# Hybrid decoder step: memory attention of the sampled sequences, eight sequences of a head in one step instead of four

## The chip, the cores and the metric

The kernel runs on one core of a Trainium2 chip. A time is the device time of one execution in microseconds; the comparison is of medians over several executions. The profile is of one execution of its own. Engines are called PE (matrix products), DVE (vector), ACT (scalar, activations), POOL and SP (here only an issuer of DMAs).

## What is computed

One decoding step of a two-layer decoder for two request groups with the same weights: one prompt of 512 tokens and eight sampled sequences of 8 tokens. Each layer has a mixer, a cross-attention into 256 memory tokens, and a feed-forward part. The change touches the cross-attention of the sampled group (`q` is 8 x 8 x 4 heads x 256, `k` and `v` are caches of 8 x 256 x 4 x 256, one for each sequence):

```python
def mem_attend(h, k, v, w_q, w_o):
    B, T, _ = h.shape
    q = (h @ w_q).reshape(B, T, MEM_HEADS, MEM_HEAD_DIM)
    s = jnp.einsum('bthe,bnhe->bhtn', q, k, preferred_element_type=F32) * MEM_HEAD_DIM ** -0.5
    p = jax.nn.softmax(s, axis=-1)
    o = jnp.einsum('bhtn,bnhe->bthe', p, v.astype(F32)).reshape(B, T, D_MODEL).astype(h.dtype)
    return o @ w_o
# in every layer
xp = xp + mem_attend(rmsnorm(xp, g_mem_q[layer]), mk, mv, w_mem_q[layer], w_mem_o[layer])
xs = xs + mem_attend(rmsnorm(xs, g_mem_q[layer]), cache_mem_k[layer], cache_mem_v[layer],
                     w_mem_q[layer], w_mem_o[layer])
```

## The kernel before, in words

The whole step is one program. The prompt's 512 columns and the samples' 64 stand side by side, so that the dense products (`dense`, line 922) run over 256 and 320 columns (`HALF`, line 32). A dense weight comes as a raw 128x1024 tile `wr`; ACT casts its high part `wh`, DVE subtracts the low part `wl` (`low_now`, line 891), and each product is made of three matmuls (`wh` twice, `wl` once). There are two raw buffers (`NR`, line 709): the load of the weight after next (`load_to`, line 857) is issued on SP's queue and waits there until DVE has made the `wl` of two weights earlier, which reads the same buffer.

The memory stage `mem_stage` (line 1891) runs once in each layer. The planner `sched` (line 802) writes its instructions in one order for all engines. Into the dense product of Q (the filler) and then the dense product of the output (`o`, which waits in the planner until all parts of its head are in `fin`), it lays three lanes, piece by piece: the prompt's attention in two halves (`mem_prompt`, line 1927, four heads each), and the samples' attention (`mem_sample`, line 1974), a chain of eight steps: four heads, two blocks of four sequences each. PE takes its instructions in exactly the written order, and so does each other engine. The numbers that a piece yields are its estimated time on PE and until its next piece may follow.

One step of `mem_sample` takes four K tiles; makes S in one PSUM bank, with four sequences side by side in groups of 32 rows (8 matmuls of 256 columns); takes the row maximum on DVE; the exponential on ACT; turns P on PE and copies it out; takes four V tiles; makes P V (8 matmuls); scales on ACT; turns the result back; and splits it for the output product.

K and V come through a `_Stream` (line 440): a list of sources (`mem_src`, line 1923, K of a block then V of it) from which tiles of 128x512 (256 KB) are loaded on SP's queue, up to eight ahead (`get`, `fill`), but a further one only where the arena has more than `MROOM` = 4500 columns of room left (line 308). Tiles lie in regions of large pages, which get new owners when the old tile is deleted: a load waits on SP until the last reader of its region is done. All DMAs of the stage go through SP's queue in the written order.

Of the kernel before, what the change touches and what calls it, by code (L numbers as in the profile page):

```python
# [11 lines left out]
AF = mybir.ActivationFunctionType  # L12
OP = mybir.AluOpType
AX = mybir.AxisListType
# [293 lines left out]
MROOM = 4500  # L308
# [393 lines left out]
class _Prog:  # L702
# [1188 lines left out]
    def mem_stage(self, l, nx):  # L1891
        nc = self.nc
        Q = self.wide("mq", dt=F32)
        oh, ol = self.wide("xh"), self.wide("xl")
        done = set()

        def ev(i, hf, ps):
            t0, N = HALF[hf]
            nx.upto(hf)
            nc.vector.tensor_tensor(Q[i][:, t0:t0 + N], ps[:, :N], nx.R[:, t0:t0 + N], op=OP.mult)  # L1900
            done.add((i, hf))
            if len(done) == 2 * KT:
                nx.clear()

        q = lambda: self.dense(self.pos[f"mq{l}"], 8, KT, nx.h, nx.l, ev, first=6)

        fin = set()
        st = _Stream(self, [s for h in range(4) for k in range(2) for s in self.mem_src(l, h, k)], "Kb", 8, MROOM)
        lanes = [self.chain(*[self.mem_prompt(l, h, hf, Q, done, oh, ol, fin) for h in range(4)]) for hf in range(2)]
        lanes.append(self.chain(*[self.mem_sample(l, h, b, Q, done, st, oh, ol, fin) for h in range(4) for b in range(2)]))  # L1910
        nn = _Next(self, "g_ffn", l * 8)
        ready = lambda k: lambda: sum((k // 2, j) in fin for j in ("a0", "a1", "s0", "s1")) == 4

        def o():
            yield 0, 0, lambda: len(done) == 2 * KT
            yield from self.dense(self.pos[f"mo{l}"], 8, KT, oh, ol, self.res_evac(nn), first=6, ready=ready)

        f = self.sched(lanes + [o()], q(), METM)
        assert f is None or next(f, None) is None
        self.Kc[l], self.Vc[l] = None, None  # L1920
        return nn

    def mem_src(self, l, h, blk):
        b = range(blk * 4, blk * 4 + 4)
        return [self.aps["cmk"][l, i, h] for i in b] + [self.aps["cmv"][l, i, h] for i in b]

    def mem_prompt(self, l, h, hf, Q, done, oh, ol, fin):
        nc = self.nc
# [42 lines left out]
        fin.add((h, f"a{hf}"))  # L1971
        yield 1.7, 0

    def mem_sample(self, l, h, blk, Q, done, st, oh, ol, fin):

        nc = self.nc
        yield 0, 0, lambda: (2 * h, 1) in done and (2 * h + 1, 1) in done
        q0 = 512 + 32 * blk
        mx, den = self.T([128, 1], "mx"), self.T([128, 1], "den")
        Kb = [st.get() for _ in range(4)]  # L1980
        ps = self.PS()
        for eh in range(2):
            for j in range(4):
                c = q0 + 8 * j - 24
                nc.tensor.matmul(ps[32 * j:32 * j + 32, :256], Q[2 * h + eh][:, c:c + 32],
                                 Kb[j][:, eh * 256:eh * 256 + 256], start=eh == 0, stop=eh == 1)
        del Kb
        nc.vector.tensor_reduce(mx[:], ps[:, :256], axis=AX.X, op=OP.max)
        nc.vector.tensor_scalar(mx[:], mx[:], -1.0 / 16, None, op0=OP.mult)
        yield 1.0, 1.0  # L1990
        p_ = self.S([128, 256], s="P")
        nc.scalar.activation(p_[:], ps[:, :256], AF.Exp, bias=mx[:], scale=1.0 / 16, accum_out=den[:])
        del ps
        yield 0, 0.9
        ps = self.PS()
        for kt in range(2):
            nc.tensor.transpose(ps[:, kt * 128:kt * 128 + 128], p_[:, kt * 128:kt * 128 + 128], self.ident)
        pt = self.S([128, 256], s="PT")
        nc.vector.reciprocal(den[:], den[:])
        nc.vector.tensor_copy(pt[:], ps[:, :256])  # L2000
        yield 0.22, 1.2
        Vb = [st.get() for _ in range(4)]
        O = self.PS()
        for kt in range(2):
            for j in range(4):
                nc.tensor.matmul(O[32 * j:32 * j + 32, :256], pt[:, kt * 128 + 32 * j:kt * 128 + 32 * j + 32],
                                 Vb[j][:, kt * 256:kt * 256 + 256], start=kt == 0, stop=kt == 1)
        del Vb
        o = self.S([128, 256], s="O")
        nc.scalar.activation(o[:], O[:, :256], AF.Copy, scale=den[:])  # L2010
        yield 1.0, 1.2
        ps = self.PS()
        for vh in range(2):
            nc.tensor.transpose(ps[:, vh * 128:vh * 128 + 128], o[:, vh * 128:vh * 128 + 128], self.ident)
        for vh in range(2):
            i = 2 * h + vh
            v = lambda a: a.rearrange("p (j c) -> p j c", j=4)
            src = v(ps[:, vh * 128:vh * 128 + 128])[:, :, 24:32]
            self.split(src, v(oh[i][:, q0:q0 + 32]), v(ol[i][:, q0:q0 + 32]))
        fin.add((h, f"s{blk}"))  # L2020
        yield 0.22, 0


    def ffn(self, l, nx, nn):
# [476 lines left out]
```

## Time and profile before

| what | value |
|---|---|
| three runs | 2065.84, 2068.98, 2069.39 us; median 2068.98 us |
| the profiled execution | 2069.16 us, of which the span of its instructions is 2067.4 us |
| PE, DVE, ACT busy | 97%, 61%, 39% of the span |
| the chain that ended last | PE 87%, DVE 6%, DMA 3%, ACT 3% |
| mean granted TensorE clock | 0.989 of full speed |
| K and V tiles of the memory stages | 128 loads of 256 KB, 5.2 us (K) and 4.9 us (V) from issue to landing |

All instructions are recorded in one helper line, L630, so rows are told apart by tiles: `page,wh` and `page,wl` are dense products, `page,page 128*32` are the samples' S or P V (a row of 16 records is the eight matmuls of a group), `page,page 128*128` the prompt's, and `cid,page` the turnings. A timeline row gives its start, its length and in brackets the idle time before it. Rows overlap a little at their ends, so that the time of a group is better read from its start to the next row's start. SPq is SP's queue of DMA issues.

### The profile page before, as it was taken

The page shows a single profiled execution, that of the slowest core. Times are in us where ns is not written, and L with a number is a line of the kernel's source. Part 1 is how long each engine was busy: PE and PEld are TensorE (multiplying, and loading weights), DVE is VectorE, ACT ScalarE, POOL GpSimd, SP SyncE. Part 2 cuts the span into 40 slices and gives each one's busy share as a digit, 9 for nine tenths or more (in the row PEclk, how much of TensorE's full clock was granted, in tenths as well). Part 3 has the DMA queues.
Part 4 walks back from the last instruction along what each step waited for, and adds up shares of the span by engine and source line. Part 5 has one row for each costly group of instructions (what it writes and reads, how often), then busy time and mean ns, then how long its engine had stood idle before and what let it go on. Part 6 is the DMA issues. An engine that isn't in the chain of part 4 may idle for free.

```text
span 2067.4 us, 40636 instructions
## 1 busy us (share of the span) xinstructions
PE 2010.5 (97%) x16443; PEld 1860.1 (90%) x16443; DVE 1259.5 (61%) x3020; ACT 801.3 (39%) x1674; POOL 264.6 (13%) x570
## 2 busy tenths in 40 slices
PE   7999999999999999999999999999999999999997
PEld 6999867978999999999898878878879999999996
DVE  7785676643677377377426666655645675575575
ACT  5554434333444244144322342344434443343342
POOL 1142120000012012020003212200000021121111
PEclk9999999999999999999999999999999999999998
DMA  4222145555222222222555555566453222222222
GB/s 150 69 65 73 54 123 190 189 184 186 79 83 82 82 82 82 83 83 88 156 185 169 181 178 194 182 205 199 168 190 113 79 82 86 85 86 83 82 70 77
DMA packets 104092, 252.30 MB, mean 122 GB/s; under 512 B 11169, under 2 KB 22049, under 8 KB 103905
## 3 DMA queue, kind: packets, MB, share of 16 engines
q1 hardware_dynamic: 103760, 249.49, 37.1%
q8 instruction: 129, 2.11, 0.4%
q14 instruction: 59, 0.48, 0.1%
q10 hardware_dynamic: 144, 0.22, 0.0%
HBM read 227.70 MB, written 21.96 MB: 121 GB/s over the span
## 4 chain that ended last, share of the span: by engine, by line
PE 87%; DVE 6%; DMA 3%; ACT 3%; issue 1%; POOL 0%; SPq 0%; DVEq 0%; ACTq 0%; POOLq 0%
PE p L630 87%; DVE page L630 4%; ACT page L630 2%; DMA wr<-in_w 1%; DVE wl L630 1%; ACT wh L630 1%; DMA page<-in_cmk 1%; DVE rn L630 1%; DMA out_o_ss<-page 0%; DMA page<-xd 0%; DMA page<-in_x 0%; POOL page L630 0%; SPq L630 0%; DMA xd<-page 0%; DVE ot L630 0%
## 5 line engine op out<-in xcount | busy, mean ns | idle before, releaser
L630 PE MATMUL p<-page,wh 128*128 128x256 f32 (+1 forms) x7296 | 1103.1, 299 | 17.6 <-ACT wh L630 12.8
L630 PEld LDWEIGHTS p<-page,wh 128*128 128x128 f32 x7296 | 1012.9, 191 | 45.9 <-issue 20.6
L630 PE MATMUL p<-page,wl 128*128 128x256 f32 (+1 forms) x3648 | 589.7, 298 | 0.0
L630 PEld LDWEIGHTS p<-page,wl 128*128 128x128 f32 x3648 | 519.7, 191 | 14.0 <-issue 13.1
L630 DVE TENSOR_TENSOR page<-p,page 128x256 f32<-128x256 f32 (+5 forms) x647 | 242.1, 392 | 320.0 <-PE p L630 233.2
L630 ACT CAST wh<-wr 128x1024 fp32r<-128x1024 f32 (+1 forms) x268 | 275.6, 1031 | 391.9 <-PE p L630 313.6
L630 DVE TENSOR_TENSOR wl<-wr,wh 128x1024 fp32r<-128x1024 f32 (+1 forms) x268 | 332.9, 1245 | 83.5 <-ACT wh L630 76.7
L630 DVE SCALAR_TENSOR_TENSOR page<-page,vecs,page 128x256 f32<-128x256 f32 (+4 forms) x545 | 283.9, 526 | 97.7 <-ACT page L630 86.8
L630 PE MATMUL p<-page,page 64*64 64x64 f32 (+12 forms) x3778 | 296.7, 298 | 11.5 <-DVE page L630 4.0
L630 PEld LDWEIGHTS p<-page,page 128*32 128x32 f32 (+6 forms) x3778 | 191.1, 130 | 80.1 <-issue 30.4
L630 ACT ACTIVATE page<-page,vecs 128x256 f32<-128x256 f32 (+5 forms) x319 | 169.1, 539 | 229.7 <-DVE page L630 223.7
L630 POOL COPY page<-page 128x16 f32<-128x16 f32 (+5 forms) x312 | 128.6, 438 | 731.2 <-DVE page L630 731.2
L630 ACT ACTIVATE page<-page 128x256 f32<-128x256 f32 (+6 forms) x293 | 116.2, 412 | 139.0 <-DVE page L630 132.7
L630 POOL TENSOR_TENSOR page<-page,page 128x256 f32<-128x256 f32 (+6 forms) x93 | 90.1, 976 | 463.1 <-DVE page L630 325.9
L630 ACT COPY page<-p 128x256 f32<-128x256 f32 (+8 forms) x161 | 63.9, 413 | 186.2 <-PE p L630 185.3
L630 PE MATMUL p<-wh,page 128*128 128x512 f32 (+1 forms) x368 | 119.1, 397 | 0.0
L630 DVE TENSOR_TENSOR page<-page,page 128x256 fp32r<-128x256 f32 (+8 forms) x178 | 80.1, 462 | 57.8 <-ACT page L630 56.8
L630 DVE TENSOR_TENSOR page<-page 128x256 f32<-128x256 f32 (+5 forms) x225 | 99.4, 454 | 16.3 <-POOL page L630 11.1
L630 ACT CAST page<-page 128x256 fp32r<-128x256 f32 (+2 forms) x118 | 50.4, 442 | 125.7 <-DVE page L630 125.7
L630 PEld LDWEIGHTS p<-wh,page 128*128 128x128 f32 (+1 forms) x368 | 77.3, 223 | 14.4 <-issue 2.5
L630 PE MATMUL p<-cid,page 128*128 128x128 f32 (+3 forms) x669 | 79.4, 258 | 5.7 <-ACT page L630 4.0
L630 POOL MEMSET page<- 128x2 f32 (+4 forms) x110 | 12.2, 112 | 539.2 <-PE p L630 290.1
(84 smaller groups left out, 827.5 us busy)
## 6 DMA issues: line engine op xcount, KB each, us to landing
wr<-in_w SPq DMA_DIRECT2D x252, 512.0 KB, 3.6
page<-in_ck SPq DMA_DIRECT2D x72, 256.0 KB, 4.6
page<-in_cv SPq DMA_DIRECT2D x72, 256.0 KB, 4.2
page<-in_cmk SPq DMA_DIRECT2D x64, 256.0 KB, 5.2
page<-in_cmv SPq DMA_DIRECT2D x64, 256.0 KB, 4.9
wr<-in_w SPq DMA_DIRECT2D x16, 384.0 KB, 3.1
xd<-page SPq DMA_DIRECT2D x16, 288.0 KB, 4.3
out_o_v<-page SPq DMA_DIRECT2D x12, 256.0 KB, 4.3
```

Of the source, the lines that this page charges most:

```text
L630: return f(*args, **kw)
```

## The change

The two blocks of a head become one step. `mem_sample` takes eight K tiles, then makes both blocks' S in the two halves of one PSUM bank (16 matmuls), with one maximum of 128x2 over 512 columns, two exponentials, four turnings in place of two and a copy of 512 columns; then it takes eight V tiles and makes both blocks' P V (16 matmuls), two scaled copies, four turnings and a split of 64 columns. The stream's order becomes eight K then eight V for each head, in place of four and four; `ahead` and `MROOM` stay. The output product waits in the planner for one part `s` instead of `s0` and `s1`. PE has as many instructions as before; DVE has 48 fewer and ACT 16 fewer; SP has as many DMAs.

```diff
--- before.py
+++ after.py
@@ -1905,11 +1905,11 @@
         q = lambda: self.dense(self.pos[f"mq{l}"], 8, KT, nx.h, nx.l, ev, first=6)
 
         fin = set()
-        st = _Stream(self, [s for h in range(4) for k in range(2) for s in self.mem_src(l, h, k)], "Kb", 8, MROOM)
+        st = _Stream(self, [s for h in range(4) for s in self.mem_src(l, h)], "Kb", 8, MROOM)
         lanes = [self.chain(*[self.mem_prompt(l, h, hf, Q, done, oh, ol, fin) for h in range(4)]) for hf in range(2)]
-        lanes.append(self.chain(*[self.mem_sample(l, h, b, Q, done, st, oh, ol, fin) for h in range(4) for b in range(2)]))
+        lanes.append(self.chain(*[self.mem_sample(l, h, Q, done, st, oh, ol, fin) for h in range(4)]))
         nn = _Next(self, "g_ffn", l * 8)
-        ready = lambda k: lambda: sum((k // 2, j) in fin for j in ("a0", "a1", "s0", "s1")) == 4
+        ready = lambda k: lambda: sum((k // 2, j) in fin for j in ("a0", "a1", "s")) == 3
 
         def o():
             yield 0, 0, lambda: len(done) == 2 * KT
@@ -1920,9 +1920,8 @@
         self.Kc[l], self.Vc[l] = None, None
         return nn
 
-    def mem_src(self, l, h, blk):
-        b = range(blk * 4, blk * 4 + 4)
-        return [self.aps["cmk"][l, i, h] for i in b] + [self.aps["cmv"][l, i, h] for i in b]
+    def mem_src(self, l, h):
+        return [self.aps["cmk"][l, i, h] for i in range(8)] + [self.aps["cmv"][l, i, h] for i in range(8)]
 
     def mem_prompt(self, l, h, hf, Q, done, oh, ol, fin):
         nc = self.nc
@@ -1971,54 +1970,64 @@
         fin.add((h, f"a{hf}"))
         yield 1.7, 0
 
-    def mem_sample(self, l, h, blk, Q, done, st, oh, ol, fin):
+    def mem_sample(self, l, h, Q, done, st, oh, ol, fin):
+
 
         nc = self.nc
         yield 0, 0, lambda: (2 * h, 1) in done and (2 * h + 1, 1) in done
-        q0 = 512 + 32 * blk
-        mx, den = self.T([128, 1], "mx"), self.T([128, 1], "den")
-        Kb = [st.get() for _ in range(4)]
+        mx, den = self.T([128, 2], "mx"), self.T([128, 2], "den")
+        Kb = [st.get() for _ in range(8)]
         ps = self.PS()
-        for eh in range(2):
-            for j in range(4):
-                c = q0 + 8 * j - 24
-                nc.tensor.matmul(ps[32 * j:32 * j + 32, :256], Q[2 * h + eh][:, c:c + 32],
-                                 Kb[j][:, eh * 256:eh * 256 + 256], start=eh == 0, stop=eh == 1)
+        for b in range(2):
+            for eh in range(2):
+                for j in range(4):
+                    c = 512 + 32 * b + 8 * j - 24
+                    nc.tensor.matmul(ps[32 * j:32 * j + 32, b * 256:b * 256 + 256], Q[2 * h + eh][:, c:c + 32],
+                                     Kb[4 * b + j][:, eh * 256:eh * 256 + 256], start=eh == 0, stop=eh == 1)
         del Kb
-        nc.vector.tensor_reduce(mx[:], ps[:, :256], axis=AX.X, op=OP.max)
+        nc.vector.tensor_reduce(mx[:], ps[:].rearrange("p (b n) -> p b n", b=2), axis=AX.X, op=OP.max)
         nc.vector.tensor_scalar(mx[:], mx[:], -1.0 / 16, None, op0=OP.mult)
-        yield 1.0, 1.0
-        p_ = self.S([128, 256], s="P")
-        nc.scalar.activation(p_[:], ps[:, :256], AF.Exp, bias=mx[:], scale=1.0 / 16, accum_out=den[:])
+        yield 2.0, 1.2
+        p_ = self.S([128, 512], s="P")
+        for b in range(2):
+            c = slice(b * 256, b * 256 + 256)
+            nc.scalar.activation(p_[:, c], ps[:, c], AF.Exp, bias=mx[:, b:b + 1], scale=1.0 / 16, accum_out=den[:, b:b + 1])
         del ps
-        yield 0, 0.9
+        yield 0, 1.2
         ps = self.PS()
-        for kt in range(2):
-            nc.tensor.transpose(ps[:, kt * 128:kt * 128 + 128], p_[:, kt * 128:kt * 128 + 128], self.ident)
-        pt = self.S([128, 256], s="PT")
+        for n in range(4):
+            nc.tensor.transpose(ps[:, n * 128:n * 128 + 128], p_[:, n * 128:n * 128 + 128], self.ident)
+        pt = self.S([128, 512], s="PT")
         nc.vector.reciprocal(den[:], den[:])
-        nc.vector.tensor_copy(pt[:], ps[:, :256])
-        yield 0.22, 1.2
-        Vb = [st.get() for _ in range(4)]
+        nc.vector.tensor_copy(pt[:], ps[:])
+        del p_
+        yield 0.44, 1.2
+        Vb = [st.get() for _ in range(8)]
         O = self.PS()
-        for kt in range(2):
-            for j in range(4):
-                nc.tensor.matmul(O[32 * j:32 * j + 32, :256], pt[:, kt * 128 + 32 * j:kt * 128 + 32 * j + 32],
-                                 Vb[j][:, kt * 256:kt * 256 + 256], start=kt == 0, stop=kt == 1)
+        for b in range(2):
+            for kt in range(2):
+                for j in range(4):
+                    c = b * 256 + kt * 128 + 32 * j
+                    nc.tensor.matmul(O[32 * j:32 * j + 32, b * 256:b * 256 + 256], pt[:, c:c + 32],
+                                     Vb[4 * b + j][:, kt * 256:kt * 256 + 256], start=kt == 0, stop=kt == 1)
         del Vb
-        o = self.S([128, 256], s="O")
-        nc.scalar.activation(o[:], O[:, :256], AF.Copy, scale=den[:])
-        yield 1.0, 1.2
+        o = self.S([128, 512], s="O")
+        for b in range(2):
+            c = slice(b * 256, b * 256 + 256)
+            nc.scalar.activation(o[:, c], O[:, c], AF.Copy, scale=den[:, b:b + 1])
+        yield 2.0, 1.2
         ps = self.PS()
         for vh in range(2):
-            nc.tensor.transpose(ps[:, vh * 128:vh * 128 + 128], o[:, vh * 128:vh * 128 + 128], self.ident)
+            for b in range(2):
+                nc.tensor.transpose(ps[:, vh * 256 + b * 128:vh * 256 + b * 128 + 128],
+                                    o[:, b * 256 + vh * 128:b * 256 + vh * 128 + 128], self.ident)
         for vh in range(2):
             i = 2 * h + vh
-            v = lambda a: a.rearrange("p (j c) -> p j c", j=4)
-            src = v(ps[:, vh * 128:vh * 128 + 128])[:, :, 24:32]
-            self.split(src, v(oh[i][:, q0:q0 + 32]), v(ol[i][:, q0:q0 + 32]))
-        fin.add((h, f"s{blk}"))
-        yield 0.22, 0
+            v = lambda a: a.rearrange("p (j c) -> p j c", j=8)
+            src = v(ps[:, vh * 256:vh * 256 + 256])[:, :, 24:32]
+            self.split(src, v(oh[i][:, 512:576]), v(ol[i][:, 512:576]))
+        fin.add((h, "s"))
+        yield 0.44, 0
 
 
     def ffn(self, l, nx, nn):
```

What it moves, first on SP in head 1 of layer 0. `page_3939` and `page_4197` are the pages with the stream's regions, `wr_…` the raw weights. Before:

```order
L630 DMA wr_4793<-in_w 128x1024
L630 DMA wr_4806<-in_w 128x1024
L630 DMA page_3939<-in_cmk 128x512 x3
L630 DMA page_3939<-in_cmv 128x512 x4
L630 DMA page_4197<-in_cmk 128x512
L630 DMA wr_4975<-in_w 128x1024
L630 DMA page_3939<-in_cmk 128x512 x3
L630 DMA page_3939<-in_cmv 128x512 x4
L630 DMA page_4197<-in_cmk 128x512
```

After:

```order
L630 DMA wr_4808<-in_w 128x1024
L630 DMA page_3939<-in_cmk 128x512 x7
L630 DMA page_4197<-in_cmk 128x512
L630 DMA page_4197<-in_cmv 128x512
L630 DMA wr_4970<-in_w 128x1024
L630 DMA page_3939<-in_cmv 128x512 x7
L630 DMA wr_5047<-in_w 128x1024
```

Before, three K and four V tiles stand between two weight loads, for blocks that come later. Now eight K tiles of head 1 stand ahead of the first V tile of that head, the load of `wr_4970` comes next, and the head's other seven V tiles behind it.

DVE at the same place: `mx` is the row maximum (`mx_4910` and `mx_4928` that of the samples), `wl_4858` and `wl_4882` the low part whose raw buffer `wr_4970` and `wr_4975` take. Before:

```order
L630 TENSOR_REDUCE mx_4919<-p_4921 128x2
L630 TENSOR_SCALAR mx_4919<-mx_4919 128x2
L630 TENSOR_REDUCE mx_4928<-p_4935 128x1
L630 TENSOR_SCALAR mx_4928<-mx_4928 128x1
L630 TENSOR_TENSOR wl_4882<-wr_4793,wh_4881 128x1024
L630 RECIPROCAL den_4920<-den_4920 128x2
L630 TENSOR_SCALAR page_4197<-page_4197,den_4920 128x256 x2
L630 RECIPROCAL den_4929<-den_4929 128x1
```

After:

```order
L630 TENSOR_REDUCE mx_4901<-p_4903 128x2
L630 TENSOR_SCALAR mx_4901<-mx_4901 128x2
L630 TENSOR_REDUCE mx_4910<-p_4921 128x2
L630 TENSOR_SCALAR mx_4910<-mx_4910 128x2
L630 TENSOR_TENSOR wl_4858<-wr_4791,wh_4857 128x1024
L630 RECIPROCAL den_4902<-den_4902 128x2
L630 TENSOR_SCALAR page_4197<-page_4197,den_4902 128x256 x2
```

The order is the same; the samples' maximum is of two blocks now, and the low part stands right behind it, as it did.

PE at the start of head 3, layer 0. Before, `p_5444` is the prompt's S of head 3 and `p_5464` the samples' S of its first block, which reads K from three pages:

```order
L630 MATMUL p_5444<-page_2397,page_4458 128x256 x4
L630 MATMUL p_5464<-page_4197,page_4458 32x256
L630 MATMUL p_5464<-page_3939,page_4458 32x256 x2
L630 MATMUL p_5464<-page_5453,page_4458 32x256
L630 MATMUL p_5464<-page_4197,page_4458 32x256
L630 MATMUL p_5464<-page_3939,page_4458 32x256 x2
L630 MATMUL p_5464<-page_5453,page_4458 32x256
L630 MATMUL p_5475<-page_4459,wh_5142 128x256
```

After, `p_5379` is the prompt's P V, which reads P from `page_4197`; `p_5356` dense; `p_5399` the prompt's S of head 3, and `p_5426` the samples' S, with K in `page_5408` alone:

```order
L630 MATMUL p_5379<-page_4197,page_2398 128x256 x4
L630 MATMUL p_5356<-page_4192,wl_4943 128x320 x4
L630 MATMUL p_5356<-page_4193,wl_4943 128x320 x4
L630 MATMUL p_5399<-page_2397,page_4458 128x256 x4
L630 MATMUL p_5426<-page_5408,page_4458 32x256 x16
L630 MATMUL p_5448<-page_4459,wh_5105 128x256
```

The samples' S is of 16 matmuls and reads one page. SP at that place after the change, from head 2's V tiles on:

```order
L630 DMA page_3939<-in_cmv 128x512 x7
L630 DMA wr_5295<-in_w 128x1024
L630 DMA page_5408<-in_cmk 128x512 x8
L630 DMA page_5408<-in_cmv 128x512
L630 DMA page_5418<-in_cmv 128x512 x7
L630 DMA wr_5471<-in_w 128x1024
```

SP there before the change:

```order
L630 DMA wr_5325<-in_w 128x1024
L630 DMA page_3939<-in_cmk 128x512 x2
L630 DMA page_5453<-in_cmk 128x512
L630 DMA page_5453<-in_cmv 128x512 x3
L630 DMA page_5458<-in_cmv 128x512
L630 DMA page_5458<-in_cmk 128x512 x3
L630 DMA page_3939<-in_cmk 128x512
L630 DMA wr_5500<-in_w 128x1024
```

All eight K tiles of head 3 lie in `page_5408` now, a page newly laid over the memory of a retired one; before, a new page (`page_5453`) took one of the first three K tiles behind a weight load, and the others went to regions of the old page.

## Rows read from the trace of the kernel before

**Rows 1.** The page, part 1: busy us (share of span) xinstructions of each engine.
```profile
PE 2010.5 (97%) x16443; PEld 1860.1 (90%) x16443; DVE 1259.5 (61%) x3020; ACT 801.3 (39%) x1674; POOL 264.6 (13%) x570
```

**Rows 2.** Windows of both memory stages: busy (x) by engine, PEclk, DMA share.
```profile
415.00:525.00 110.00, 107.82 (x831) 87.59 (x830) 44.63 (x126) 35.73 (x104) 0.00 (x0) 1.00 0.49 169
1470.00:1580.00 110.00, 105.98 (x815) 85.71 (x814) 43.93 (x123) 35.25 (x102) 0.00 (x0) 1.00 0.50 173
```

**Rows 3.** Timeline of PE, head 1, layer 0: start, us, group of instructions.
```profile
451.79 2.18 PE L630 MATMUL p<-page,wh 128*128 128x256 f32 x16
...
455.34 0.72 PE L630 MATMUL p<-page,wh 128*128 128x256 f32 x4
455.99 1.07 PE L630 MATMUL p<-page,page 128*32 128x256 f32 x16
456.99 0.50 PE L630 MATMUL p<-page,wh 128*128 128x256 f32 x2
457.33 1.89 PE L630 MATMUL p<-page,page 128*128 128x256 f32 x8
459.05 0.38 PE L630 MATMUL p<-cid,page 128*128 128x128 f32 x2
459.36 2.44 PE L630 MATMUL p<-page,page 128*32 128x256 f32 x16
461.73 1.45 PE L630 MATMUL p<-page,wh 128*128 128x256 f32 x10
```

**Rows 4.** Timeline of PE, layer 1, K waits; idle and releaser in brackets.
```profile
1515.68 1.05 PE L630 MATMUL p<-page,page 128*32 128x256 f32 x10 [0.59 <-DMA page<-in_cmk]
...
1544.72 1.05 PE L630 MATMUL p<-page,page 128*32 128x256 f32 x10 [1.30 <-DMA page<-in_cmk]
```

**Rows 5.** Timeline of DVE, head 1, layer 0.
```profile
450.90 0.69 DVE L630 TENSOR_REDUCE mx<-p 128x2 f32<-128x512 f32 x1 [1.65 <-PE p L630]
...
451.93 0.42 DVE L630 TENSOR_REDUCE mx<-p 128x1 f32<-128x256 f32 x1
...
452.46 1.22 DVE L630 TENSOR_TENSOR wl<-wr,wh 128x1024 fp32r<-128x1024 f32 x1
```

**Rows 6.** Timeline of SP's DMA issues, the weight load after those DVE rows.
```profile
453.74 0.33 SPq L630 DMA_DIRECT2D wr<-in_w  x1
```

**Rows 7.** SP's issues in layer 1, the weight load ahead of seven tiles.
```profile
1508.86 0.33 SPq L630 DMA_DIRECT2D wr<-in_w  x1
```

**Rows 8.** Tile in_cmk, the first three tiles behind it; issue to landing.
```profile
L630 SPq DMA_DIRECT2D page<-in_cmk x3: 382/422/424, 1509.3 to 1510.2; - x3
...
DMA to landing us min/median/max: 3.8/4.0/5.4
```

**Rows 9.** Tile in_cmv, the last four tiles behind that load.
```profile
L630 SPq DMA_DIRECT2D page<-in_cmv x4: 328/398/430, 1510.7 to 1512.2; - x4
...
DMA to landing us min/median/max: 5.7/5.9/6.1
```

**Rows 10.** Timeline of SP, the first four K tiles of layer 0's stage.
```profile
407.08 1.85 SPq L630 DMA_DIRECT2D page<-in_cmk  x4
```

**Rows 11.** Tile in_cmv, the four V tiles issued behind them.
```profile
L630 SPq DMA_DIRECT2D page<-in_cmv x4: 432/432/577, 409.0 to 410.6; - x4
...
DMA to landing us min/median/max: 5.7/5.9/6.0
```

**Rows 12.** Timeline of PE, head 3, layer 0: low-part matmuls of 320 columns.
```profile
502.69 1.34 PE L630 MATMUL p<-page,wl 128*128 128x320 f32 x8
```

**Rows 13.** Timeline of PE outside the stage, a hole of 1.92 us.
```profile
277.18 1.12 PE L630 MATMUL p<-page,page 64*128 64x512 f32 x2 [1.92 <-POOL page L630]
```

**Rows 14.** Windows behind that hole, and around another sparse stretch.
```profile
279.40:282.90 3.50, 3.50 (x20) 3.17 (x23) 1.18 (x5) 0.07 (x1) 0.00 (x0) 0.51 0.74 283
336.00:340.90 4.90, 2.85 (x13) 1.81 (x12) 3.59 (x9) 3.36 (x8) 0.34 (x1) 1.00 0.84 281
340.90:351.10 10.20, 8.64 (x30) 7.30 (x31) 6.81 (x16) 4.54 (x13) 0.00 (x0) 0.50 0.76 266
```

## The prediction

> **What bounds the kernel now.** I read the page's busy times first. PE is busy 97% of the span, DVE 61%, ACT 39% [rows 1]. Then I looked at the two stages in which the changed code runs. In 110 us of each, PE works 107.8 and 106.0 us at a granted clock of 1.00, while DVE works 45 and ACT 36 us [rows 2]. So the stage is bound by PE in its written order: work taken from DVE and ACT is worth nothing by itself, and what counts is what PE's sequence costs and whether PE has to stand still for data. The reader should look for that in PE's timeline. In head 1 of layer 0 one group follows the next without a hole, with a single exception: the second block's S group takes from 459.36 to 461.73, 2.37 us, where a group that has its data takes 455.99 to 456.99, 1.00 us [rows 3]. In layer 1 two such groups stop in their midst for 0.59 and 1.30 us, released by K tiles [rows 4]. So K loads already come late at three places, and DMA stands close behind PE here: the DMA engines are half busy in the stages [rows 2].
>
> **The change, part by part.** I sum against the profiled execution, 2069.16 us (span 2067.4); the median of the runs, 2068.98, is the same within 0.2.
>
> *Fewer groups on PE: a gain.* The matmuls stay; 32 groups of S and P V in two layers become 16 of twice the size. What a group costs beside its matmuls is seen at its edges. Sixteen dense matmuls take 2.18 and ten take 1.45, so one takes 0.122. The four dense ones from 455.34 to 455.99 should take 0.49 and take 0.65: 0.16 for the turn into the group [rows 3]. I take as much again for the turn out, an estimate: 0.3 for each of 16 groups that go, 4.8 us; bounds 2.6 (the turn in alone) and 5. The turnings, two before and four now, and the copies stay at nothing, since PE turns something else meanwhile.
>
> *The K waits of before: a gain.* K tiles of a head are now asked for as soon as the V matmuls of the head before have read their regions, some ten us ahead. The three waits go: 1.37 + 0.59 + 1.30 = 3.3 us [rows 3, 4]. With both gains and nothing else the time is 2069.2 - 4.8 - 3.3 = 2061.1.
>
> *DVE and ACT.* One maximum over 512 columns takes 0.69 where one over 256 took 0.42 [rows 5]; the exponentials and the scaled copies are the same instructions, and engines with 60 us to spare in 110 hide them. The 0.27 us only counts below, in the wait of a weight load.
>
> *Where V lies in the stream: a loss.* The stream's room is some eight or nine tiles, and it stays so. Before, a step held four K tiles, and four or five more (its V) were on their way. Now a step holds all eight K, so at most one V tile fits beside them. The other seven V tiles take the regions of K, and can't be issued before PE's S matmuls have read them. The order on SP shows it: eight K and one V of head 1 stand in a row, then comes the weight load `wr_4970`, and the other seven V behind it. That load is what decides in heads 1 and 2 of both layers. It waits for the low part `wl_4858`, which stands on DVE behind the maximum of this very S group. So the seven V tiles start after S, maximum and low part. I count from T, the start of the dense matmuls behind the S group (451.79 in rows 3). Before, the same weight load went out at 453.74 [rows 6], just after the low part's end (452.46 + 1.22 = 453.68 [rows 5]): T + 1.95; with the longer maximum T + 2.22. How long a weight and seven tiles behind it need is shown at 1508.86 [rows 7]: the third tile is issued at 1510.2 and lands up to 5.4 later, 6.7 after the weight's issue [rows 8]; the seventh is issued at 1512.2 and lands 6.1 later, 9.4 after [rows 9]. So the eighth V tile lands at T + 11.6. Behind it PE still has five of the sixteen matmuls, 0.6 us: T + 12.2. Undisturbed, the P V group would come after 24 dense matmuls (2.9), eight turnings (0.8: two take 0.31 from 459.05 to 459.36), ten more dense (1.2), the prompt's P V (457.33 to 459.05, 1.72) and a turn (0.16), at T + 6.8, and end 1.9 later at T + 8.7 [rows 3]. PE loses 3.5 us, four times: **14.0 us**. Bounds for one: 2.8 (no longer maximum, landing in 5.7) and 4.7 (DVE has one more operation of the size of a low part, 1.22, ahead of it [rows 5]). PE can do nothing else meanwhile: the dense matmuls stand behind the group in its queue.
>
> The Trainium skill, "DMA: Bandwidth & Descriptors", section "Anatomy of one DMA — SWDGE (gpsimd) path", fits a transfer at 2.0 us and the bytes at 436 GB/s. By it a weight and seven tiles (2.36 MB) would take 7.4 us where the rows show 9.4 [rows 7, 9], an estimate; each of the four stalls would then be 2.0 us smaller and the sum 8 us lower. It is for another way of issuing, and I go by the row.
>
> *Head 3, both layers.* All eight K tiles go into a page newly opened, over memory that the prompt's P held last; the first K load waits until the prompt's P V of head 2 (`p_5379`) is done, call it E. The issue follows a release by 0.06 (453.68 to 453.74 [rows 5, 6]). Eight tiles in a row were issued from 407.08 [rows 10] on, the last at 410.6, landing 6.0 later: 9.4 us after the first; at seven steps of 0.432 and 5.9 it is 8.9 [rows 11]. I take 9.0, and 0.6 for the last matmuls: E + 9.6. Undisturbed, S would follow eight low-part matmuls (1.34 [rows 12]), the prompt's S (1.72, as its P V), a turn, and end at E + 5.1. So PE loses 4.5 us, twice: **9.0 us**; bounds 3.5 and 5.1 for one. In head 0 V goes out behind S without a weight ahead of it, and P V stands some 8 us behind S: I take nothing, and up to 1 us each at the upper end.
>
> Stalls: 14.0 + 9.0 = 23.0. 2061.1 + 23.0 = 2084.1.
>
> *What the holes do to the clock.* The stage has had a clock of 1.00 throughout, and its longest hole was 1.30 [rows 2, 4]. Elsewhere a hole of 1.92 us [rows 13] was followed, 2 us later, by 3.5 us at 0.51 in which PE was fully busy; and 4.9 us in which PE did only 2.85 were followed by 10.2 us at 0.50 [rows 14], which is 1.2 GHz. At half clock half the stretch is lost: 1.75 and 5.1 us. The six new holes are 3.5 to 4.5 us with little work between the landings, so they are longer than the one and much like the other. If three in four take the clock, at the mean of the two prices (3.4), each costs 2.5: **15 us**; bounds 0 and 30.6. Sum: 2084.1 + 15 = **2099**.
>
> **Rivals.**
>
> *Stalls, but the clock stays up.* Each landing tile lets PE run two matmuls, so a stall is a row of small holes below the 1.92 that cost the clock; 1.30 did not [rows 2, 4]. Against it: 2.85 busy us of 4.9 did [rows 14]. It gives 2084, 2079 with the low bounds of the stalls (4 x 2.8 + 2 x 3.5 = 18.2).
> The Trainium skill, "TensorE: Matmul & The Clock Gate", section "HAM oscillation — how this bites in real kernels", has the clock fall where PE waits on DMA, idle, across a window, and paid for anew at each wait; by it a stall that is broken by matmuls would not take the clock, which is this rival. The trace agrees only in part: the hole of 1.92 us was enough [rows 13].
>
> *V comes in time, and it is faster.* The place is the V group of heads 1 and 2. If the eighth V tile landed by T + 8.1, 3.5 us earlier than I have it, the group would not wait: it would need the weight load not to wait for the low part, or a transfer rate of seven tiles in less than 6 us. Then, with head 3's K loaded some 4.5 us earlier too, only the gains are left: 2061, from 2059 to 2067. For it: DMA is only half busy on average [rows 2]. Against it: the order on SP, and 9.4 us for the like row of loads.
>
> *The same.* Stalls of about 8 us (a third of my sum) would just eat the gains: 2069.
>
> *Deeper.* Each hole takes the clock at the upper price, or half-speed PE delays the next low part and so the next V: 2084 + 30.6 = 2115.
>
> **How the numbers follow.** Chances: the forecast, with some loss of clock (2088 to 2114) 0.60; stalls alone (2078 to 2088) 0.22; above 2114 0.06; the same, 0.04; V in time and faster, 0.08. The range from 2079 to 2114 leaves out these last three and a rest at its lower edge, under 2 in 10. A measurement of this kernel tells some 0.2% (4 us) from no change. Faster 0.08, same 0.04, slower 0.88.
>
> **What would show it.** In PE's timeline after the change, holes released by in_cmv ahead of or within the 32-record groups of heads 1 and 2, about 3.5 us each, and by in_cmk in head 3, about 4.5 us; on SP, the weight load ahead of seven V tiles issued some 2.2 us after T; behind the holes windows of a granted clock of 0.50. The P V groups of head 0 without a hole. The three waits of before gone, and groups that have their data at about 1.9 us. The prediction is wrong if the V tiles are issued ahead of the weight load or land within 6 us of it, if the DMA holes sum to less than 15 us, or if the clock stays at 1.00 through both stages.

## The result, and the profile after

The changed kernel takes 2083.85 us (median of 4 runs, 2083.42 to 2083.91); the kernel before 2067.41 (4 runs, 2062.36 to 2069.39). The ratio is 1.008, with an interval from 1.0065 to 1.0094: **slower by 16.4 us**. The forecast was 2099 in a range from 2079 to 2114; the time is that of the first rival, the stalls without the clock, 2084. It lies in the range because the range was laid down to this rival; the forecast itself was 15 us too high.

The page of the profiled execution (span 2081.6 us), first its busy times, then the chain that ended last by engine:

```profile
PE 2017.8 (97%) x16443; PEld 1862.3 (89%) x16443; DVE 1253.7 (60%) x2972; ACT 797.7 (38%) x1658; POOL 265.7 (13%) x570
...
PE 85%; DVE 6%; DMA 4%; ACT 3%; issue 1%; SPq 1%; POOL 0%; DVEq 0%; ACTq 0%; POOLq 0%
```

PE works 7 us more than in [rows 1], and DMA, 3% before, has 4% of the chain. Of the two memory stages, as in [rows 2] (length, busy time and count of PE, PEld, DVE, ACT and POOL, granted clock, DMA share, GB/s):

```profile
407.00:530.00 123.00, 114.62 (x849) 92.06 (x848) 42.45 (x103) 35.02 (x96) 0.10 (x1) 1.00 0.47 166
1465.00:1590.00 125.00, 118.17 (x858) 93.68 (x858) 48.07 (x136) 35.58 (x96) 0.10 (x1) 1.00 0.49 169
```

The clock is 1.00 in both, and PE stands or waits 8.4 and 6.8 us in them, as against 2.2 and 4.0 in [rows 2]. Head 1 of layer 0 on PE, to be held against [rows 3] (start, length, group; idle time and releaser in brackets):

```profile
447.49 2.17 PE L630 MATMUL p<-page,wh 128*128 128x256 f32 x16
...
452.52 1.89 PE L630 MATMUL p<-page,page 128*128 128x256 f32 x8
454.34 0.40 PE L630 MATMUL p<-page 128*32 128x256 f32 x1
...
455.94 0.40 PE L630 MATMUL p<-page,page 128*32 128x256 f32 x1 [0.69 <-DMA page<-in_cmv]
...
456.19 3.45 PE L630 MATMUL p<-page,page 128*32 128x256 f32 x20
459.57 0.98 PE L630 MATMUL p<-page,wh 128*128 128x256 f32 x6
...
463.11 1.56 PE L630 MATMUL p<-page,page 128*128 128x256 f32 x6 [0.72 <-DVE page L630]
```

From the start of the dense matmuls behind S, T = 447.49, the P V group starts at T + 6.85 and ends at T + 12.1: 5.22 us to the next row's start, where an undisturbed group of 32 takes 1.86 (the S groups of this trace). It is broken by one idle time of 0.69, and the row of 20 that takes 3.45 is itself slow: matmuls wait in it for tiles, and each leaves less idle time than a row shows. SP at that place, and the seven tiles of that row (count, issue durations, first and last issue; landing):

```profile
449.76 0.33 SPq L630 DMA_DIRECT2D wr<-in_w  x1
450.18 3.23 SPq L630 DMA_DIRECT2D page<-in_cmv  x7
```

```profile
L630 SPq DMA_DIRECT2D page<-in_cmv x7: 382/382/382, 450.2 to 453.0; - x7
...
DMA to landing us min/median/max: 3.7/4.9/5.5
```

The weight load goes out at T + 2.27, the last of the seven tiles at 453.02, and the chain of waits takes its transfer to 458.54, T + 11.05:

```profile
453.02 5.52 DMA page<-in_cmv
...
458.59 3.14 PE p L630 x26
```

Head 3 of layer 0. The first row holds six records of the prompt's S and, from 508.39 on, the first four of the samples' S, since a row is named for its first record. S ends where 514.93 starts, 6.54 us after its start, 4.7 more than 1.86. Below it stand its eight K tiles on SP:

```profile
506.90 2.12 PE L630 MATMUL p<-page,page 128*128 128x256 f32 x10 [0.58 <-DVE page L630]
510.12 2.58 PE L630 MATMUL p<-page,page 128*32 128x256 f32 x16 [1.10 <-DMA page<-in_cmk]
513.28 1.72 PE L630 MATMUL p<-page,page 128*32 128x256 f32 x12 [0.58 <-DMA page<-in_cmk]
514.93 1.34 PE L630 MATMUL p<-page,wh 128*128 128x256 f32 x9
```

```profile
504.80 3.65 SPq L630 DMA_DIRECT2D page<-in_cmk  x8
```

**The whole account.** Both programs have the same matmuls in the same order on both sides of the stages, so the stage of layer 0 is the same 1200 PE records in both traces and that of layer 1 the same 1100. I gave each record the time until the next one starts and added these up by kind (us, before and after):

| kind of PE record | layer 0 | layer 1 | change |
|---|---|---|---|
| the samples' S and P V | 17.42, 27.29 | 19.28, 27.52 | +18.1 |
| the prompt's S and P V | 31.17, 33.30 | 31.20, 33.33 | +4.3 |
| dense, turnings, the rest | 113.13, 110.24 | 99.69, 96.96 | -5.6 |
| sum | 161.72, 170.83 | 150.17, 157.81 | +16.75 |

Outside the stages the profiled execution is 2.5 us shorter: 2.8 less ahead of layer 0's stage, 0.3 more behind it. Of the samples' 18.1, the stalls are 25.0: what groups of 32 take beyond 1.86, that is 3.36, 4.35, 4.16 and 3.30 in heads 1 and 2, 4.68 and 4.13 in head 3, and 1.03 in head 0 of layer 1. The idle times in brackets on rows released by in_cmv and in_cmk add up to only 6.3: for the rest of a stall a tile lands every 0.65 to 0.7 us or so and lets one or two matmuls through, whose records of 0.4 us fill most of that time. The K waits of before gave back 4.7, and sixteen pairs at 1.86 instead of 2 x 1.00 gave 2.2.

### The profile page after: what moved, and what is told of

Its sections match the earlier page's. It is cut to its first block, busy times and chain, and to the rows that moved or that the text cites. A ratio compares the mean times of both kernels' runs of the same rounds, so it can differ in the third digit from the quotient of the medians.

```text
span 2081.6 us, 40548 instructions
## 1 busy us (share of the span) xinstructions
PE 2017.8 (97%) x16443; PEld 1862.3 (89%) x16443; DVE 1253.7 (60%) x2972; ACT 797.7 (38%) x1658; POOL 265.7 (13%) x570
## 4 chain that ended last, share of the span: by engine, by line
PE 85%; DVE 6%; DMA 4%; ACT 3%; issue 1%; SPq 1%; POOL 0%; DVEq 0%; ACTq 0%; POOLq 0%
PE p L630 85%; DVE page L630 4%; ACT page L630 2%; DMA wr<-in_w 1%; DMA page<-in_cmv 1%; DVE wl L630 1%; ACT wh L630 1%; SPq L630 1%; DVE rn L630 1%; DMA page<-in_cmk 1%; DMA out_o_ss<-page 0%; DMA page<-xd 0%; POOL page L630 0%; DMA page<-in_x 0%; ACT L630 0%
## 5 line engine op out<-in xcount | busy, mean ns | idle before, releaser
L630 DVE TENSOR_TENSOR page<-p,page 128x256 f32<-128x256 f32 (+3 forms) x631 | 239.6, 397 | 326.5 <-PE p L630 235.5
L630 PE MATMUL p<-page,page 64*64 64x64 f32 (+12 forms) x3662 | 290.7, 297 | 20.3 <-DVE page L630 8.9
L630 PEld LDWEIGHTS p<-page,page 128*32 128x32 f32 (+6 forms) x3662 | 185.8, 129 | 93.9 <-issue 23.9
L630 POOL TENSOR_TENSOR page<-page,page 128x320 f32<-128x320 f32 (+6 forms) x106 | 100.6, 955 | 461.0 <-DVE page L630 330.8
L630 DVE TENSOR_TENSOR page<-page,page 128x256 fp32r<-128x256 f32 (+9 forms) x197 | 94.2, 486 | 62.3 <-ACT page L630 56.7
L630 DVE TENSOR_TENSOR page<-page 128x256 f32<-128x256 f32 (+4 forms) x206 | 85.2, 431 | 11.5 <-POOL page L630 6.0
L630 PE MATMUL p<-wl,page 128*128 128x512 f32 (+1 forms) x184 | 72.8, 396 | 2.3 <-DVE wl L630 2.1
```

What stands on the lines that cost most here:

```text
L630: return f(*args, **kw)
```

## The experiments

One line each, medians and the ratio to the kernel before on the same chip. The stage sums are those of the table above (before 161.72 and 150.17).

| kernel | median us (runs) | ratio, interval | stage sums, layer 0 and 1 |
|---|---|---|---|
| vfill | 2069.76 (10) | 1.0019 (1.0004 to 1.0033) | 163.25, 150.20 |
| kfill | 2074.57 (10) | 1.0040 (1.0027 to 1.0054) | 165.95, 156.15 |
| kvfill | 2054.03 (4) | 0.9941 (0.9922 to 0.9960) | 158.80, 145.07 |
| kvfill2 | 2054.88 (6) | 0.9938 (0.9923 to 0.9953) | 160.19, 145.69 |
| kvfill3 | 2054.33 (5, one of them 10943.85 and left out of the ratio) | 0.9933 (0.9920 to 0.9947) | not taken: the profile is of that one |
| room | 2055.03 (8) | 0.9950 (0.9937 to 0.9964) | 158.55, 145.21 |
| bfill | 2060.66 (11) | 0.9966 (0.9957 to 0.9975) | 160.10, 146.70 |
| vrev | 2094.42 (4) | 1.0140 (1.0114 to 1.0166) | 176.97, 164.80 |
| kvlate | 2053.15 (6) | 0.9932 (0.9917 to 0.9948) | 156.66, 142.60 |
| kvlate2 | 2053.90 (5) | 0.9928 (0.9915 to 0.9942) | 158.10, 143.30 |

The kernel before had medians of 2066.38, 2067.01 and 2067.52 in the three sets.

**vfill: V ahead of the weight load.** One line is added to the changed kernel:

```diff
         del Kb
+        st.fill(8)
```

> The changed kernel with one line more: after S, as soon as the eight K tiles are let go, the stream is filled again, so that the seven V tiles of heads 1 and 2 stand on SP ahead of the weight load that used to precede them. Theory: the stalls of heads 1 and 2 (3.3 to 4.4 us each in the trace after, 15.2 in all) come from that weight load, which waits for the low part on DVE; without it seven V tiles go out at the end of S and the eighth lands some 8 us later, about when P V wants it: stalls of 0 to 1 us each, 2069 to 2073 us, head 3 as before (4.1 to 4.7 us). Rival: V is late because K's regions come free late and the transfers are slow, whatever stands between: 2080 to 2084. Second rival: the weight load, now behind seven tiles, comes late itself and PE waits for its dense product: the V holes go and holes of in_w or wh of like size come: 2080 or more.

2069.76 us, in the range of the first theory. The seven V tiles go out where S ends, and two weight loads behind them:

```profile
448.17 3.70 SPq L630 DMA_DIRECT2D page<-in_cmv  x7
451.96 3.24 SPq L630 DMA_DIRECT2D wr<-in_w  x2
```

The P V group of head 1 runs through, 32 matmuls in 1.86 (its last 19 and the dense ones behind them):

```profile
456.48 0.38 PE L630 MATMUL p<-page 128*32 128x256 f32 x1
...
457.67 0.98 PE L630 MATMUL p<-page,wh 128*128 128x256 f32 x6
```

Of heads 1 and 2 in both layers, one group of four is 0.38 longer than 1.86, the others not at all; head 3 keeps 4.8 and 4.4 us. The weights, issued later, cost no hole. So the stalls of heads 1 and 2 came from the place behind the waiting weight load, and the tiles' rate alone was not enough to make V late.

**kfill: the next K ahead of everything, V left as it was.**

```diff
         del Vb
+        st.fill(8)
```

> The changed kernel with the stream filled again only after the V tiles are let go: the next head's K tiles stand on SP right behind P V, but heads 1 and 2 keep the weight load ahead of their seven V tiles. Theory: the two causes are independent; head 3's stalls (4.7 and 4.1 us) go, heads 1 and 2 keep theirs (15.2 us): 2074 to 2077. Rival: one DMA queue behind both, so that K tiles loaded earlier push the weights and V later and the stalls only move: 2080 or more.

2074.57 us, in the expected range. All S groups take 1.86, head 3's too; the P V groups of heads 1 and 2 keep 3.3, 4.1, 4.3 and 6.5 us. The two causes are independent. The 6.5 is a stall of another look, which returns below: one whole hole of 2.15 us, and behind it a granted clock of 0.57, mostly 1.2 GHz, where PE's records fill 3.86 of 4.00 us:

```profile
1545.04 0.67 PE L630 MATMUL p<-page 128*32 128x256 f32 x2 [2.15 <-DMA page<-in_cmv]
```

```profile
1538.00:1545.00 7.00, 4.89 (x33) 3.92 (x31) 3.49 (x8) 1.33 (x3) 0.00 (x0) 1.00 0.46 137
1545.00:1549.00 4.00, 3.86 (x18) 1.19 (x18) 0.00 (x0) 0.00 (x0) 0.00 (x0) 0.57 1.01 366
```

**kvfill: both lines.** The version that beats both kernels.

> As vfill, and filled again after the V tiles are let go too, so that the next head's eight K tiles stand on SP right behind P V, some 15 us ahead of their use, and head 3's K gets regions of the old page instead of a new page over the prompt's P. Theory: head 3's stalls (4.7 and 4.1) come from the late K loads behind the prompt's P V; they go too: 2060 to 2065 us, below the kernel before. Rival: two weight loads now wait behind eight tiles each, and PE stops for weights: 2068 or more.

2054.03, and in two more sets 2054.88 and 2054.33: 12 to 13 us below the kernel before, 30 below the change as it was, and 6 below the expected range. All sixteen groups of the profiled execution take 1.86. Of the expected fall of 24 us below the changed kernel the stages show 24.8 (328.64 to 303.87). Against the kernel before the stages are 8.0 us shorter (311.89 to 303.87), and the medians 12.4. The other 4 us lie outside the stages. The two profiled executions differ there by more than the medians do, 7.9 us: 2.6 ahead of layer 0's stage, 2.9 between the stages and 2.4 behind layer 1's. The granted clock falls at other times there from one execution to the next; whether the change of the stages has a part in that was not tried and stays open. What is left in the stage is the wait on DVE at the prompt's S:

```profile
455.55 0.38 PE L630 MATMUL p<-page 128*32 128x256 f32 x1
...
456.74 0.98 PE L630 MATMUL p<-page,wh 128*128 128x256 f32 x6
...
460.28 1.56 PE L630 MATMUL p<-page,page 128*128 128x256 f32 x6 [0.72 <-DVE page L630]
```

> kvfill again, beside the other two on one chip: 2052 to 2056.

The repetition shows how far one execution is from another: 2.0 us in the stages, 0.75 and 0.32 of it in two P V groups.

**room: more room instead of an earlier request.**

```diff
-MROOM = 4500
+MROOM = 500
```

> The changed kernel with the reserve of the arena, MROOM, at 500 columns instead of 4500, so that V tiles of a head are loaded ahead of S beside the eight K tiles. Theory: all stalls (25 us in the trace after) come from the missing room for V; with it V and K are there in time, and 2058 to 2065 us are left. Rival: the planner's other tiles then lie in other pages and loads wait for these instead: 2070 to 2084.

2055.03 us, 3 below the expected range; all groups 1.86, stage sums as kvfill's within 0.3. The eight V tiles of head 1 now stand on SP ahead of its S, which starts at 446.17, and of the weight load:

```profile
431.26 11.63 SPq L630 DMA_DIRECT2D page<-in_cmv  x8
450.22 0.33 SPq L630 DMA_DIRECT2D wr<-in_w  x1
```

So it was the reserve that turned eight held K tiles into late V tiles.

**bfill: the two lines in the kernel before,** in its `mem_sample` of four sequences.

> The kernel before (blocks of four, as it was) with the stream filled again as soon as K and V tiles are let go. Theory: its three K waits (4.6 us in the trace before) come from the same late filling and go: some 4.5 us under the kernel before. Then what kvfill is below this kernel is what the merging itself brings, 3.7 us by the records (7.9 less for group edges, turnings and their neighbours, 4.2 more in waits for DVE). Rival: the filling gives the whole of kvfill's 12 us, and the merging nothing.

2060.66 us, some 6 us under the kernel before, where 4.5 were expected. In the stages 5.1 us go, 4.7 of them in the samples' groups, all of which take 1.00 now. kvfill2, measured beside it, is another 6 us lower in the medians, clear of the scatter. In the stages it is 0.9 lower (306.80 to 305.88), and kvfill's first profiled execution 2.9 (303.87). So the merging itself is a small gain, once its loads are in time, and half of kvfill's gain over the kernel before has nothing to do with it. The stages show 1 to 3 of the 6 us; where the rest comes from stays open.

**vrev: a whole hole instead of a broken one.**

```diff
-        return [self.aps["cmk"][l, i, h] for i in range(8)] + [self.aps["cmv"][l, i, h] for i in range(8)]
+        return [self.aps["cmk"][l, i, h] for i in range(8)] + [self.aps["cmv"][l, i, h] for i in range(7, -1, -1)]
...
-        Vb = [st.get() for _ in range(8)]
+        Vb = [st.get() for _ in range(8)][::-1]
```

> The changed kernel with the V tiles loaded in reverse order, so that the tile that P V needs first lands last: in heads 1 and 2 one whole hole of some 4.2 us takes the place of holes of 0.2 to 1.4 us between matmuls; P V ends some 0.8 us later each, 3 us in all. Theory that the clock stayed up because the holes were broken by matmuls: the granted clock falls to 0.5 behind some of the four whole holes, at 1.75 to 5.1 us each as in the kernel before: 2092 to 2107. Rival, that such holes in this stage don't take the clock: 2087, clock 1.00 in both stages.

2094.42 us, in the range of the first theory. The profile is of the slowest of its four executions (2100.91; the others 2091.36 to 2095.63). P V can't begin before its last tile, and PE stands still in one piece:

```profile
461.71 2.35 PE L630 MATMUL p<-page,page 128*32 128x256 f32 x19 [4.61 <-DMA page<-in_cmv]
...
495.80 1.54 PE L630 MATMUL p<-page,page 128*32 128x256 f32 x19 [4.34 <-DMA page<-in_cmv]
...
1535.65 2.35 PE L630 MATMUL p<-page,page 128*32 128x256 f32 x19 [4.01 <-DMA page<-in_cmv]
...
1569.94 2.36 PE L630 MATMUL p<-page,page 128*32 128x256 f32 x19 [3.98 <-DMA page<-in_cmv]
```

In each of the four the clock falls (windows from inside the hole to some us behind it; the seventh figure is the granted clock):

```profile
457.00:465.00 8.00, 3.39 (x33) 1.57 (x32) 0.85 (x2) 0.74 (x2) 0.00 (x0) 0.63 0.58 217
492.00:501.00 9.00, 5.20 (x47) 3.87 (x48) 0.75 (x2) 1.21 (x3) 0.00 (x0) 0.81 0.46 175
1533.00:1541.00 8.00, 5.35 (x40) 3.36 (x41) 0.37 (x1) 0.84 (x2) 0.00 (x0) 0.58 0.47 167
1567.00:1576.00 9.00, 6.06 (x46) 4.10 (x47) 0.42 (x1) 1.06 (x3) 0.00 (x0) 0.62 0.38 148
```

The windows hold stretches at 0.50 and the rest at 1.00. Against them, three of the six stalls of the changed kernel, like in length, with the same instructions:

```profile
454.30:459.60 5.30, 4.46 (x34) 1.48 (x33) 0.85 (x2) 0.74 (x2) 0.00 (x0) 1.00 1.01 376
485.40:491.60 6.20, 4.45 (x34) 1.44 (x33) 0.85 (x2) 0.74 (x2) 0.00 (x0) 1.00 0.75 288
508.40:515.00 6.60, 4.79 (x34) 1.51 (x33) 0.86 (x2) 1.02 (x4) 0.00 (x0) 1.00 0.98 368
```

The clock stays at 1.00, in the other three stalls too. Each tile that lands lets some matmuls through, and no whole hole is longer than 1.35 us. By the records PE is busy 4.5 to 4.8 us of 5.3 to 6.6 though the 32 records could pass in 1.86: each record lasts 0.38 to 0.40 whether its matmul waited or not, so that the two or so which a tile lets through fill most of the time to the next landing.

**kvlate: the DVE waits.** In kvfill, the low halves of the attention's last splits are written ten dense steps later in heads 0 to 2:

```diff
-        for vh in range(2):
-            self.split(ps[:, vh * 256:vh * 256 + 256], oh[2 * h + vh][:, d], ol[2 * h + vh][:, d])
-        fin.add((h, f"a{hf}"))
+        self.split_late(LATE if h < 3 else 0, [(ps[:, vh * 256:vh * 256 + 256], oh[2 * h + vh][:, d], ol[2 * h + vh][:, d])
+                                               for vh in range(2)], lambda: fin.add((h, f"a{hf}")))
...
+    def split_late(self, n, parts, end):
+        for src, h, _ in parts:
+            self.nc.scalar.copy(h, src)
+        def low():
+            for src, h, l in parts:
+                self.nc.vector.tensor_tensor(l, src, h.bitcast(F32), op=OP.subtract)
+            end()
+        if n:
+            self.later(n, low)
+        else:
+            low()
```

`LATE` is 10, and the samples' split is changed in the same way.

> kvfill with the DVE halves of the attention's last splits (the low parts for the output product) written ten dense steps later in heads 0 to 2. Theory: the ten waits of the prompt's S on DVE (0.58 to 0.88 us, 7.6 in all, 4.2 more than before) come from Q's evacuation standing on DVE behind these splits, which wait for ACT; they go, and 4 to 7 us with them: 2047 to 2050. Rival: the waits are the evacuation's own time behind the last dense matmul, and stay: 2054.

What it was about, in the changed kernel: DVE, then PE at the same place.

```profile
442.40 0.42 DVE L630 TENSOR_TENSOR page<-p,page 128x256 fp32r<-128x256 f32 x1 [4.71 <-ACT page L630]
443.26 0.82 DVE L630 TENSOR_TENSOR page<-p,page 128x256 fp32r<-128x256 f32 x2 [0.44 <-ACT page L630]
```

```profile
442.66 0.59 PE L630 MATMUL p<-page,page 128*128 128x256 f32 x2
444.13 2.13 PE L630 MATMUL p<-page,page 128*128 128x256 f32 x14 [0.88 <-DVE page L630]
```

The row at 443.26 is two operations: the second low half of 0.42, which waited 0.44 for ACT, and behind it the evacuation of Q from 443.60 on, 0.48. Its matmuls had ended at 442.66 or soon after; the prompt's S can go on only at 444.13. In kvlate the evacuation stands alone on DVE, and PE's wait is 0.15:

```profile
447.87 0.49 DVE L631 TENSOR_TENSOR page<-p,page 128x320 f32<-128x320 f32 x1 [5.17 <-PE p L631]
```

```profile
447.67 0.59 PE L631 MATMUL p<-page,page 128*128 128x256 f32 x2
448.41 1.92 PE L631 MATMUL p<-page,page 128*128 128x256 f32 x10 [0.15 <-DVE page L631]
```

The mechanism is right: of the ten waits, 7.6 us, six are left at 0.15 to 0.33, and the prompt's matmuls take 30.3 us in each stage, less than before the change. But 2053.15 us is outside the expected 2047 to 2050 and nearer to the rival's 2054. Of the 6.0 us won there, 4.6 remain in the stages of one execution and 2.5 in those of the other, against kvfill's first. Part of the rest stands in new waits: in heads 1 and 2 the turnings now wait for DVE, 0.24 to 0.30 each, 1.1 in all:

```profile
455.19 1.14 PE L631 MATMUL p<-cid,page 128*128 128x128 f32 x8 [0.29 <-DVE page L631]
```

In the other execution a wait for DVE ahead of the attention (1.75 at 398.93, where kvfill has 0.53) takes another 1.2.

> kvlate once more. In the profiled executions its two memory stages are 4.6 us shorter than kvfill's first one, while the medians of six runs each were 1.7 us apart, with executions scattered over 6 us. Theory: the stages' gain reaches the end, and the medians differ by 3 to 5 us when more runs are counted. Rival: something behind the stage waits longer and takes part of it: 0 to 2 us.

The median of all fourteen runs of kvfill (one of 10.9 ms left out) is 2054.25, that of eleven of kvlate 2053.77. The expected 3 to 5 us are not there, and this expectation failed too; whether 0 or 2 us remain, the scatter of executions over 6 us doesn't tell.

## Why the prediction was right, and where it was not

*The order on SP, heads 1 and 2: right, in each step.* The weight load went out at T + 2.27 (2.22 forecast), the eighth V tile landed at T + 11.05 in head 1 and T + 12.05 in head 2 (11.6), P V began at T + 6.85 (6.8) and ended at T + 12.1 and 13.1 (12.2). The stalls are 15.2 us in sum for 14.0. vfill shows the cause: the place behind the weight load. The last tile landed 8.8 us after the weight's issue in head 1 and 9.75 in head 2, against 9.4 by the row. The fit of the Trainium skill ("DMA: Bandwidth & Descriptors", "Anatomy of one DMA — SWDGE (gpsimd) path") is for one transfer issued another way; worked out for these bytes it gives an estimate of 7.4, and the trace doesn't agree with it for loads that follow one another on SP's queue.

*Head 3: right.* 4.68 and 4.13 for 4.5 each; eight tiles landed 9.1 us after the first issue (9.0). kfill shows that the late request is the cause.

*Head 0:* nothing in layer 0 and 1.03 in layer 1, at the bound of 1.

*Gains: mis-sized.* The K waits gave 4.7 for 3.3: I had counted in layer 1 the idle time alone and not the shorter waits beside it, though the one in layer 0 was counted whole. The edges of groups gave up to 7.8 (2.2 in the groups, 5.6 in the dense matmuls and turnings) for 4.8, above the bound of 5. Of the 5.6, 0.8 are two waits ahead of the attention, which differ from one execution to the next.

*What was missing: waits on DVE, a loss of 4.3.* "The turnings ... and the copies stay at nothing" and "engines with 60 us to spare in 110 hide them" overlooked that the planner moves other work when the samples' pieces get bigger. The prompt's P V now stands right ahead of the end of a dense product, so Q's evacuation queues on DVE behind two splits that wait for ACT, and the prompt's S waits for Q. The time that DVE had to spare said nothing of its order. The rows on the order in the text ahead showed head 1's maximum and low part, not this place.

*The stalls without the clock, 2084.1 for 2083.85:* closer than its terms, and that is luck: the gains were up to 4.4 too small, the DVE waits of 4.3 were missing, and the two cancel. The stalls were 2.0 too small (25.0 for 23.0). By the stages it is +16.75 for +14.9.

*The clock: wrong.* The step that failed is "much like the other": I likened the stalls to the stretch with 2.85 busy of 4.9 [rows 14], and they are like the K waits of before [rows 4]. The prediction had named a clock of 1.00 through both stages as a sign that it is wrong, and that sign came true: the 15 us were not lost. (By the bracketed idle times alone, 6.3 us, its sign on the sum of the holes would have come true as well; by the time from start to start it did not.) The price itself was near: vrev, with whole holes of 4.0 to 4.6 us, has stages 13.1 us longer than the changed kernel's (341.77 and 328.64). Behind the ends of the four holes the clock stays at 0.50 for 4.3, 3.4, 5.5 and 5.4 us; half of that is 9.3, or 2.3 for each hole where 2.5 were forecast. Of the other 3.8, 1.8 are longer waits in heads 0 and 3, and the rest is P V starting later. By the medians vrev is 10.6 us above the changed kernel; less the same 3.8 that leaves 1.7 for each hole, an estimate. Only the condition, a hole in one piece, was not met.

How long a hole must be, the runs don't settle. The place of [rows 13] has a hole in each of eleven traces (all but kvfill3's), 1.12 to 2.15 us, and the clock falls within 2.3 us behind five of them (1.57, 1.66, 1.83, 1.92, 1.98) and not behind the other six (1.12, 1.52, 1.62, 1.68, 1.97, 2.15). It stayed up behind 2.15 in kfill and fell behind 1.57 in kvfill2:

```profile
276.45 1.12 PE L630 MATMUL p<-page,page 64*128 64x512 f32 x2 [2.15 <-POOL page L630]
...
276.40:286.00 9.60, 9.55 (x67) 6.92 (x67) 5.57 (x19) 3.69 (x7) 0.00 (x0) 1.00 0.41 155
```

```profile
275.34 1.12 PE L630 MATMUL p<-page,page 64*128 64x512 f32 x2 [1.57 <-POOL page L630]
...
275.30:282.00 6.70, 6.66 (x34) 4.67 (x34) 2.24 (x8) 2.06 (x5) 0.00 (x0) 0.75 0.66 228
```

So the hole of 1.92, which the prediction took as enough, was enough in some executions only. What is shown is the contrast: four of four whole holes of 4.0 to 4.6 us took the clock, and none of thirteen broken stalls of 3.3 to 5.5 us did (six in the changed kernel, three in kfill, two each in vfill and vrev). The stretch of [rows 14], with two holes of 1.07 and 1.36 and little work around them, shows too that a single hole's length is not all. The section of the Trainium skill on which the rival drew, "TensorE: Matmul & The Clock Gate", "HAM oscillation — how this bites in real kernels", has the clock fall where PE's wait for DMA crosses a window, and paid for anew at each wait. The four whole holes agree with that; that a broken stall is spared was the rival's own inference, and the six stalls bear it out.

## What to carry to other kernels

A step that holds twice the tiles at once takes the room in which its next tiles were prefetched: before merging steps, count held plus coming tiles against the reserve, and look at what stands ahead of the reloads on the issuing queue, above all a load that waits for a compute engine. Asking for the next tiles where the old ones are let go, two lines, turned a loss of 16 us into a gain of 12, and gave the unmerged kernel half of that. Before charging a stall with a fall of the clock, see whether work trickles through it.

## What the runs showed of the hardware that was not expected

Stalls of 3.3 to 4.7 us in the changed kernel, whose longest idle time was 1.35 us, left the granted clock at 1.00; the same transfers in reverse order, one hole of 4.0 to 4.6, brought 1.2 GHz each time. Holes of 1.5 to 2.2 us at one place of the program did in some executions and not in others (2.15 not, 1.57 yes). A part of such a slow stretch lies inside the hole and costs nothing: by windows of 2 us, the clock around vrev's first hole is down from about 459.2 to 466.0, and the hole ends at 461.7, so that half of 4.3 us is lost and not half of 6.8.
